# Two transformer blocks on one core: operands of block products made in steps, a last chunk of six tiles, and ten 4 kB weight tiles

## The chip, the cores and the metric

The kernel runs on one core of a Trainium2 chip. A core has a matrix engine (PE, with its weight loads shown as PEld), a vector engine (DVE), a scalar engine (ACT), a general engine (POOL) and a queue engine (SP) that issues most DMAs. The metric is the device time of one execution in microseconds. Matmul results land in PSUM; everything else lies in SBUF, 128 partitions wide.

## The reference

Two transformer blocks in float32 on one sequence of 512 tokens, width 1024. The change touches only the two feed-forward parts of the first block and the tiles that all weights go through:

```python
def swiglu(x, w1, w3, w2):
    return (jax.nn.silu(x @ w1) * (x @ w3)) @ w2

# first block, D_MODEL 1024, D_FF 2816
f = swiglu(rms_norm(h, ffn1_pre_g), ffn1_w1, ffn1_w3, ffn1_w2)
h = h + 0.5 * rms_norm(f, ffn1_post_g)
# sparse attention, short convolution, gates and merge ("mix")
# cross attention over 256 memory rows ("cross")
f = swiglu(rms_norm(h, ffn2_pre_g), ffn2_w1, ffn2_w3, ffn2_w2)
h = h + 0.5 * rms_norm(f, ffn2_post_g)
# second block: two attentions ("mix2"), an MLP ("mlp"), a gated part ("ple"), a final norm
```

## The kernel before, in words

Everything is kept transposed: a feature tile is 128 features by 512 tokens, so h is 8 tiles. A float32 product is made from three matmuls: each operand is split into a high part (a cast to a reduced float on ACT) and a low part (a subtraction on DVE), and `mm3` multiplies high by high, high by low, and low by high.

**Weights.** `load` (lines 241 to 251) takes a raw weight tile by DMA (tag `r4`, three tiles of 4 kB), casts it on ACT (line 249) and subtracts on DVE (line 250) into two tiles of tag `w4` (eight tiles of 4 kB, so four pairs). `lead_weights` (lines 262 to 282) loads the first weights of a phase through `r4` too, but puts the parts into slots of the pools `u` and `b`. The pools of working tiles have 32 (`b`), 8 (`t`) and 5 (`u`) slots of 2 kB, and 16 for split inputs (`x`).

**A feed-forward part** (`ffn`, lines 666 to 734). `enter` and `begin` turn h into split inputs xs and a row r of reciprocal norms, the token halves A and B one after the other; the first products run per half as their inputs come. The hidden width of 2816 is 22 tiles, taken in chunks of 4, 4, 4, 4, 4 and 2. For the first chunk the products with w1 and w3 are plain: four are made in `begin` (five in the second feed-forward part), the rest in `stream`, 24 matmuls each. `up` gives each hidden tile two `t` slots and a pair of `b` slots (u). Then `forms` (lines 359 to 398) makes the seven operands of the block products from h, the gain and r: four scaled blocks of h and three sums of them, each split in high and low parts, in slots of `t` (raw values), `b` and `x` (parts). It takes 16 scalings (line 368), 8 sums (line 375), 14 casts (line 381) and 14 subtractions (line 382). All other chunks use `fast` (line 424): a product of two tiles at a time by a scheme with seven instead of eight half-size block products. `blocks` (lines 400 to 422) makes its weights: two loads (`one` in `r4`, `two` in `r6`), differences (lines 412 to 414, `three` in `r4`, `four` in `r2`), and parts in `w4` and, for `four`, `w2` (lines 419 and 420).

After each chunk `down` multiplies its u tiles by w2 into eight result tiles f: eight products of 12 matmuls for a chunk of four, of 6 for a chunk of two. The first chunk's results are copied (line 661), the others added (line 659). In the last chunk the last five of the eight products (four in the second feed-forward part) run in halves: the A halves at once, the B halves kept in `self.rest`, which `begin` of the next phase issues between its own first steps.

**Order.** The program is written as one stream of operations, and a planner puts them in order on each engine: among what is ready in its plan it takes what stands first in the program, and it hands out the tiles of a tag as they come free. Each engine then runs its list strictly in order. So a subtraction that stands behind others on DVE waits for them, whoever needs it. SP's list of loads is in order too: a load whose raw tile isn't free holds those behind it.

Each phase names by `K["lead:..."]` the pools of its leading weights: `ubbbb` is one product's parts in `u` and four products' in `b`.

Of the kernel before, what the change touches and what calls it, by code (L numbers as in the profile page):

```python
# [11 lines left out]
F32 = mybir.dt.float32  # L12
F32R = mybir.dt.float32r
I32 = mybir.dt.int32
AF = mybir.ActivationFunctionType
OP = mybir.AluOpType
# [3 lines left out]
P = 128  # L20
D = 1024
KD = D // P
S = 512
# [3 lines left out]
KF = FF // P  # L27
# [29 lines left out]
HALVES = (A, B)  # L57
# [12 lines left out]
 'lo:mix': [6],  # L70
 'lo:mix2': [],
 'work': ['a', 'a', 'a', 'b', 'vK', 'V', '0', '1', '2', '3', 'bb', 'b', 'b', '', '', 'b'],
 'sizes:ffn1': [4, 4, 4, 4, 4, 2],
 'sizes:ffn2': [4, 4, 4, 4, 4, 2],
 'plain': 4,
 'urg:ffn1sf': 0,
 'sq:ffn1sf': 'PV',
# [90 lines left out]
 'oa': 'VVVVVVVV'}  # L168
BANKS = {k: v for k, v in K["banks"].items() if v}
SLOTS = dict(zip("btu", K["slots"]))  # L170
WEIGHTS = {"r6": 2, "r4": 3, "r2": 1, "w4": 8, "w2": 2}


def width(tok):
# [3 lines left out]
class Net:  # L178
    def __init__(self, ctx, tc, a):
# [6 lines left out]

        self.wp = {t: pool(t, n) for t, n in WEIGHTS.items()}

# [152 lines left out]
        for do in todo:  # L341
            do()

    def stream(self, jobs, tail=0, spare=0):

        mid = len(jobs) - tail
        for w, n, xs, k0, put in jobs[:mid]:
            put(self.lin(self.weights(w, n, len(xs), k0)[0], xs), ALL)  # L350
        wts = [self.lead_weights(w, n, len(xs), k0, "x") if i < spare else self.weights(w, n, len(xs), k0)[0]
               for i, (w, n, xs, k0, _) in enumerate(jobs[mid:])]
        for (_, _, xs, _, put), wt in zip(jobs[mid:], wts):
            put(self.lin(wt, xs, A), A)
            self.rest.append(lambda xs=xs, put=put, wt=wt: put(self.lin(wt, xs, B), B))
# [2 lines left out]

    def forms(self, gain, r):

        nc, h = self.nc, self.h
        two = lambda alloc, dt: [alloc((P, S), dt).rearrange("p (k t) -> p k t", k=2) for _ in range(2)]
        out = {}

        def scaled(c, half, alloc=self.tmp):
            t, tok = two(alloc, F32), HALVES[half]
            for k in range(4):
                nc.vector.scalar_tensor_tensor(  # L368
                    t[k // 2][:, k % 2], h[4 * c + k][:, tok], self.g(gain, 4 * c + k), r[:, tok], op0=OP.mult, op1=OP.mult)
            return t  # L370

        def combined(x, y, op):
            t = two(self.tmp, F32)
            for o, i, j in zip(t, x, y):
                nc.vector.tensor_tensor(o, i, j, op=op)
            return t

        def parts(name, src, alloc):
            hi, lo = two(alloc, F32R), two(alloc, F32R)
            for t, i, j in zip(src, hi, lo):  # L380
                nc.scalar.copy(i, t)
                nc.vector.tensor_tensor(j, t, i.bitcast(F32), op=OP.subtract)
            out[name] = [(hi[k // 2][:, k % 2], lo[k // 2][:, k % 2]) for k in range(4)]


        b11, b12 = scaled(0, 0), scaled(0, 1)
        t1 = combined(b11, b12, OP.subtract)
        parts("11", b11, self.big)
        b21 = scaled(1, 0, lambda shape, dt: self.big(shape, dt))
        parts("21", b21, self.big)  # L390
        b22 = scaled(1, 1)
        t2 = combined(b22, t1, OP.subtract)
        parts("1", t1, self.big)
        parts("2", t2, self.xt)
        parts("22", b22, self.xt)
        parts("3", combined(b22, b12, OP.add), self.xt)
        parts("4", combined(b21, t2, OP.subtract), self.xt)
        return out

    def blocks(self, w, n):  # L400

        nc, src = self.nc, self.a[w]
        c = 4 * P

        def tiles(tag, m):
            return self.weight(tag, m * c).rearrange("p (b c) -> p b c", c=c)

        one, two, three, four = tiles("r4", 2), tiles("r6", 3), tiles("r4", 2), tiles("r2", 1)

        nc.sync.dma_start(one, src[n].rearrange("p (b k) c -> p b (k c)", b=2))  # L410
        nc.sync.dma_start(two[:, 0:2], src[n + 1].rearrange("p (b k) c -> p b (k c)", b=2))
        nc.vector.tensor_tensor(two[:, 2], two[:, 0], one[:, 0], op=OP.subtract)
        nc.vector.tensor_tensor(three, two[:, 1:2].to_broadcast([P, 2, c]), two[:, 0::2], op=OP.subtract)
        nc.vector.tensor_tensor(four[:, 0], one[:, 1], three[:, 1], op=OP.subtract)
        out = []
        for tag, raw in (("w4", one), ("w4", three), ("w2", four), ("w4", two[:, 1:3])):
            m = raw.shape[1]
            hi, lo = tiles(tag, m), tiles(tag, m)
            nc.scalar.copy(hi, raw)  # L419
            nc.vector.tensor_tensor(lo, raw, hi.bitcast(F32), op=OP.subtract)  # L420
            out += [[(hi[:, b, k * P : k * P + P], lo[:, b, k * P : k * P + P]) for k in range(4)] for b in range(m)]
        return dict(zip(("11", "12", "1", "2", "4", "22", "3"), out))
# [226 lines left out]
        self.nc.scalar.dma_start(t, self.a[name])  # L649
        return t  # L650

    def down(self, w, f, k0, xs, add, late=(0, 0)):

        nc = self.nc

        def put(n):
            def go(ps, tok):
                if add:
                    nc.vector.tensor_tensor(f[n][:, tok], f[n][:, tok], ps, op=OP.add)
                else:  # L660
                    nc.scalar.copy(f[n][:, tok], ps)
            return go

        self.stream([(w, n, xs, k0, put(n)) for n in range(KD)], *late)

    def ffn(self, pre, post, w1, w3, w2):
        self.phase = post[:4]
        nc = self.nc
        xs, r, step = self.enter(pre)
        f = [self.big(dt=F32) for _ in range(KD)]  # L670

        def up(n):
            t1, t3, u = self.tmp(), self.tmp(), self.pair()

            def first(ps, tok):
                nc.vector.tensor_tensor(t1[:, tok], ps, r[:, tok], op=OP.mult)
                nc.scalar.activation(t1[:, tok], t1[:, tok], AF.Silu)

            def second(ps, tok):
                nc.vector.tensor_tensor(t3[:, tok], ps, r[:, tok], op=OP.mult)  # L680
                nc.gpsimd.tensor_tensor(t3[:, tok], t3[:, tok], t1[:, tok], op=OP.mult)
                self.split(t3[:, tok], [t[:, tok] for t in u])

            return u, [(w1, n, xs, 0, first), (w3, n, xs, 0, second)]

        def up2(n):

            t1, t3, u = ([self.tmp(), self.tmp()] for _ in range(2)), None, [self.pair(), self.pair()]
            t1, t3 = t1

            def first(i, tok, ps, t):
                if t is not None:
                    nc.vector.tensor_tensor(t1[i][:, tok], t, ps, op=OP.add)
                if i == 0 and tok == A:
                    return
                src, at = (t1[i], ALL) if i == 0 else (t1[i], tok)
                nc.scalar.activation(t1[i][:, at], ps if t is None else src[:, at], AF.Silu)

            def second(i, tok, ps, t):
                if t is None:  # L700
                    nc.vector.tensor_tensor(t3[i][:, tok], t1[i][:, tok], ps, op=OP.mult)
                else:
                    nc.vector.tensor_tensor(t3[i][:, tok], t, ps, op=OP.add)  # L703
                    if i == 0 and tok == A:
                        return
                    at = ALL if i == 0 else tok
                    nc.vector.tensor_tensor(t3[i][:, at], t3[i][:, at], t1[i][:, at], op=OP.mult)  # L707
                if i == 0 or t is None:
                    self.split(t3[i], u[i])

            return u, [(w1, n, first), (w3, n, second)]

        c = 0
        b = None
        for size in K["sizes:" + self.phase]:
            us, jobs, quick = [], [], []
            plain = K["plain"] if c == 0 else 0
            for n in range(c, c + plain):
                u, j = up(n)
                us.append(u)  # L720
                jobs += j
            if c == 0:
                self.begin(jobs[:K["ahead:" + self.phase]], step)
                jobs = jobs[K["ahead:" + self.phase]:]
                self.stream(jobs)
                b = self.forms(pre, r)
            for n in range(c + plain, c + size, 2):
                u, j = up2(n)
                us += u
                quick += j  # L730
            self.fast(quick, b)
            self.down(w2, f, c, us, c > 0, K["late:" + self.phase] if c + size == KF else (0, 0))
            c += size
        self.leave(f, post)

# [837 lines left out]
```

## Time and profile before

| | |
|---|---|
| three runs | 2169.66 us median, 2167.13 to 2172.68 |
| profiled execution | 2171.57 us, span 2169.8 us |
| PE busy | 2056.6 us (95%), 11852 matmuls |
| weight loads (PEld) | 1774.4 us (82%) |
| DVE busy | 1488.0 us (69%), 2869 instructions |
| ACT busy | 1031.5 us (48%) |
| POOL busy | 252.0 us (12%) |
| granted PE clock, mean | 0.971 of full |
| HBM read | 182.25 MB, 85 GB/s over the span |

The first feed-forward part takes about the first 375 us of the span, "mix" follows until about 760 us, "cross" until about 940 us, the second feed-forward part until about 1318 us, and the second block the rest. A row of the timeline gives start, duration, engine, line, operation, output from input, form and count of a run of like instructions, and in brackets how long the engine had stood idle before and what released it. Names are tiles: `mm` and `lg` are PSUM banks, `b`, `t`, `u`, `x` slots of the pools, `w` a split weight, `r` a raw one, `h` the residual, `rows` a broadcast row such as r. A row of the windows gives a stretch, its length, busy time and count for PE, PEld, DVE, ACT and POOL, and then the granted PE clock, the DMA share and GB/s.

### The profile page before, as it was taken

Reading aid. Unit: us, or ns where it says so; the run is one execution under the profiler, and the core shown is the slowest. Engines: PE = TensorE matmul, PEld = TensorE weight load, DVE = VectorE, ACT = ScalarE, POOL = GpSimd, SP = SyncE. Lnnn points to the kernel's source line nnn. Section 1 sums busy time; section 2 is a strip of 40 time slices with the busy share of each in tenths; the row PEclk is TensorE's granted clock in tenths of the full one; section 3 lists DMA queues with packets and bytes.
Section 4 is the critical chain, followed back from the end, with each engine's and each line's share of the span. In section 5 each row is a group of like instructions: output and inputs, shape, how many; then the busy total and the mean of one; then the engine's idle time right before and its main releaser. Section 6 shows DMA issues by size and latency. Waiting matters only on the chain.

```text
span 2169.8 us, 30997 instructions
## 1 busy us (share of the span) xinstructions
PE 2056.6 (95%) x11852; PEld 1774.4 (82%) x11852; DVE 1488.0 (69%) x2869; ACT 1031.5 (48%) x1877; POOL 252.0 (12%) x239
## 2 busy tenths in 40 slices
PE   8799999899999989987999997998999999999997
PEld 7699998778778878986999997876778888888887
DVE  5777777799775575475777769578987663443565
ACT  5444444673563553453544445467864432222352
POOL 2000000413331310030000003122110000000011
PEclk9999999799999989988999998999999999999999
DMA  5233333212313242220333323111012323223321
GB/s 162 73 98 105 101 107 114 77 59 88 96 61 97 69 141 83 78 69 28 104 108 107 98 76 119 59 45 49 30 49 79 119 65 97 97 88 97 106 98 40
DMA packets 67157, 186.36 MB, mean 86 GB/s; under 512 B 7104, under 2 KB 16320, under 8 KB 67008
## 3 DMA queue, kind: packets, MB, share of 16 engines
q1 hardware_dynamic: 64528, 180.97, 26.5%
q10 hardware_dynamic: 2448, 3.41, 0.5%
q8 instruction: 93, 1.52, 0.3%
q14 instruction: 56, 0.46, 0.1%
q0 software_dynamic: 32, 0.00, 0.0%
HBM read 182.25 MB, written 2.10 MB: 85 GB/s over the span
## 4 chain that ended last, share of the span: by engine, by line
PE 85%; DVE 8%; ACT 3%; issue 2%; POOL 2%; DMA 0%; SPq 0%; ACTq 0%; POOLq 0%; DVEq 0%
PE mm L287 44%; PE lg L287 34%; DVE h L592 1%; PE tt L820 1%; PE tt L544 1%; PE o L834 1%; PE o L835 1%; POOL b L890 1%; PE lg L785 1%; PE lg L786 1%; DVE t L368 1%; DVE b L591 1%; DVE w L250 0%; DVE x L476 0%; ACT w L249 0%
## 5 line engine op out<-in xcount | busy, mean ns | idle before, releaser
L287 PE MATMUL mm<-x,w 128*128 128x512 f32 (+1 forms) x2808 | 606.4, 366 | 0.5 <-DVE w L250 0.5
L287 PEld LDWEIGHTS mm<-x,w 128*128 128x128 f32 x2808 | 476.2, 189 | 90.2 <-DVE w L250 1.0
L249 ACT CAST w<-r 128x1024 fp32r<-128x1024 f32 (+2 forms) x290 | 258.8, 893 | 486.5 <-PE mm L287 221.7
L287 PE MATMUL mm<-b,w 128*128 128x512 f32 (+1 forms) x2253 | 413.7, 334 | 23.2 <-ACT w L249 20.3
L287 PEld LDWEIGHTS mm<-b,w 128*128 128x128 f32 x2253 | 337.9, 190 | 74.0 <-ACT w L249 21.5
L250 DVE TENSOR_TENSOR w<-r,w 128x1024 fp32r<-128x1024 f32 (+2 forms) x288 | 297.6, 1034 | 113.6 <-ACT w L249 106.0
L287 PE MATMUL lg<-x,w 128*128 128x256 f32 (+1 forms) x2304 | 365.7, 312 | 0.0
L287 PE MATMUL lg<-b,w 128*128 128x512 f32 (+1 forms) x1725 | 342.3, 349 | 6.6 <-DVE w L250 6.4
L287 PEld LDWEIGHTS lg<-x,w 128*128 128x128 f32 x2304 | 319.8, 188 | 33.1 <-DVE t L703 2.0
L287 PEld LDWEIGHTS lg<-b,w 128*128 128x128 f32 x1725 | 279.4, 192 | 53.2 <-DVE w L250 7.8
L419 ACT CAST w<-r 128x1024 fp32r<-128x1024 f32 (+1 forms) x144 | 135.1, 945 | 111.2 <-PE mm L287 50.3
L420 DVE TENSOR_TENSOR w<-r,w 128x1024 fp32r<-128x1024 f32 (+1 forms) x144 | 155.5, 1087 | 22.7 <-ACT w L419 21.1
L472 ACT CAST b<-t 128x512 fp32r<-128x512 f32 (+1 forms) x100 | 58.7, 587 | 114.8 <-DVE t L707 33.5
L531 POOL TENSOR_TENSOR sf<-sf,sf 128x256 f32<-128x256 f32 x28 | 21.6, 771 | 788.8 <-ACT sf L525 768.5
L531 POOL TENSOR_TENSOR sh<-sh,sh 128x256 f32<-128x256 f32 x45 | 36.4, 809 | 529.0 <-ACT sh L525 526.0
L525 ACT ACTIVATE sh<-h 128x256 f32<-128x256 f32 x128 | 49.9, 411 | 51.7 <-DVE h L592 19.8
L473 DVE TENSOR_TENSOR b<-t,b 128x512 fp32r<-128x512 f32 (+1 forms) x100 | 64.2, 642 | 14.8 <-ACT b L472 14.3
L287 PE MATMUL mm<-x,b 128*128 128x256 f32 x456 | 70.2, 300 | 2.9 <-DVE t L892 2.3
L890 POOL TENSOR_TENSOR b<-b,rows 128x512 f32<-128x512 f32 x32 | 52.3, 1635 | 174.9 <-ACT b L888 174.9
L823 DVE TENSOR_TENSOR u<-tt,u 128x512 fp32r<-128x512 f32 x92 | 61.9, 683 | 13.1 <-ACT u L822 12.5
L287 PE MATMUL lg<-x,b 128*128 128x256 f32 x456 | 69.1, 295 | 0.0
L287 PEld LDWEIGHTS mm<-x,b 128*128 128x128 f32 x456 | 63.7, 206 | 3.5 <-DVE t L892 2.6
(262 smaller groups left out, 2533.4 us busy)
## 6 DMA issues: line engine op xcount, KB each, us to landing
r<-in_ffn_w SPq DMA_DIRECT2D x86, 512.0 KB, 3.6
r<-in_w_in SPq DMA_DIRECT2D x64, 512.0 KB, 3.5
r<-in_ffn_w SPq DMA_DIRECT2D x84, 256.0 KB, 2.7
r<-in_w_up SPq DMA_DIRECT2D x32, 512.0 KB, 3.5
r<-in_w_down SPq DMA_DIRECT2D x32, 512.0 KB, 3.8
r<-in_w_out SPq DMA_DIRECT2D x8, 512.0 KB, 3.4
r<-in_xattn_w_k SPq DMA_DIRECT2D x8, 512.0 KB, 3.8
r<-in_xattn_w_v SPq DMA_DIRECT2D x8, 512.0 KB, 4.1
```

The source lines that it names most:

```text
L249: nc.scalar.copy(hi, raw)
L250: self.second.tensor_tensor(lo, raw, hi.bitcast(F32), op=OP.subtract)
L287: self.nc.tensor.matmul(ps, lhsT=lhsT, rhs=rhs, start=start, stop=stop, skip_group_check=on)
L368: nc.vector.scalar_tensor_tensor(t[k // 2][:, k % 2], h[4 * c + k][:, tok], self.g(gain, 4 * c + k), r[:, tok], op0=OP.mult, op1=OP.mult)
L419: nc.scalar.copy(hi, raw)
L420: nc.vector.tensor_tensor(lo, raw, hi.bitcast(F32), op=OP.subtract)
L472: nc.scalar.copy(hi, src)
L473: nc.vector.tensor_tensor(lo, src, hi.bitcast(F32), op=OP.subtract)
L525: nc.scalar.activation(t, x, AF.Square)
L531: eng.tensor_tensor(ts[0], ts[0], t, op=OP.add)
L823: nc.vector.tensor_tensor(lo, ps[:, :n], hi.bitcast(F32), op=OP.subtract)
L890: nc.gpsimd.tensor_tensor(t[:, tok], t[:, tok], r[:, tok], op=OP.mult)
```

## The change

`forms` no longer makes all operands at once behind the plain products. It returns two lists of steps. The first six (scaled block and its sum, and the third scaled block, for each pair of tiles) are run by `stream` between the last plain products, the other eight between the eight products of the first `down`. The sums are made in place in the tiles of the raw scaled blocks, so that eight `t` slots hold all raw values. The last two chunks, of 4 and 2 tiles, become one of 6. The weight tiles become two of tag `r6`, two of `r4` and ten of `w4`; `four` and its two parts are put in slots of the pool `u`.

```diff
- 'sizes:ffn1': [4, 4, 4, 4, 4, 2],
- 'sizes:ffn2': [4, 4, 4, 4, 4, 2],
+ 'sizes:ffn1': [4, 4, 4, 4, 6],
+ 'sizes:ffn2': [4, 4, 4, 4, 6],
...
-WEIGHTS = {"r6": 2, "r4": 3, "r2": 1, "w4": 8, "w2": 2}
+WEIGHTS = {"r6": 2, "r4": 2, "w4": 10}
...
-    def stream(self, jobs, tail=0, spare=0):
+    def stream(self, jobs, tail=0, spare=0, steps=()):
         mid = len(jobs) - tail
-        for w, n, xs, k0, put in jobs[:mid]:
+        for i, (w, n, xs, k0, put) in enumerate(jobs[:mid]):
             put(self.lin(self.weights(w, n, len(xs), k0)[0], xs), ALL)
+            for _ in range(-(-len(steps) // (mid - i))):
+                steps.pop(0)()
...
     def forms(self, gain, r):
...
+        def scaled(i, kk, half):
+            t, tok = two(self.tmp, F32), HALVES[half]
+            for k in range(2):
+                n = 4 * i + 2 * kk + k
                 nc.vector.scalar_tensor_tensor(
+                    t[:, k], h[n][:, tok], self.g(gain, n), r[:, tok], op0=OP.mult, op1=OP.mult)
             return t
+        def parts(name, kk, src, alloc):
             hi, lo = two(alloc, F32R), two(alloc, F32R)
+            nc.scalar.copy(hi, src)
+            nc.vector.tensor_tensor(lo, src, hi.bitcast(F32), op=OP.subtract)
...
+        def sum_into(a, b, x, op):
+            nc.vector.tensor_tensor(raw[a], raw[b], raw[x], op=op)
+        def make(kk):
+            x, y, z, w = ((n, kk) for n in "xyzw")
+            def b11():
+                raw[x] = scaled(0, kk, 0)
+                parts("11", kk, raw[x], self.big)
+            def t1():
+                raw[y] = scaled(0, kk, 1)
+                sum_into(x, x, y, OP.subtract)
+                parts("1", kk, raw[x], self.big)
+            def b21():
+                raw[w] = scaled(1, kk, 0)
+                parts("21", kk, raw[w], self.big)
+            def b22():
+                raw[z] = scaled(1, kk, 1)
+                parts("22", kk, raw[z], self.xt)
...
+            return [b11, t1], [b21], [b22, t3, t2, t4]
+        (a, b, c), (d, e, f) = make(0), make(1)
+        return out, a + d + b + e, c + f
...
     def blocks(self, w, n):
-        one, two, three, four = tiles("r4", 2), tiles("r6", 3), tiles("r4", 2), tiles("r2", 1)
+        single = lambda dt: self.slot("u", (P, c), dt).rearrange("p (b c) -> p b c", c=c)
+        one, two, three, four = tiles("r4", 2), tiles("r6", 3), tiles("r4", 2), single(F32)
...
-            hi, lo = tiles(tag, m), tiles(tag, m)
+            hi, lo = (tiles("w4", m) if m > 1 else single(F32R) for _ in range(2))
...
-                self.stream(jobs)
-                b = self.forms(pre, r)
+                b, early, steps = self.forms(pre, r)
+                self.stream(jobs, steps=early)
...
-            self.down(w2, f, c, us, c > 0, K["late:" + self.phase] if c + size == KF else (0, 0))
+            self.down(w2, f, c, us, c > 0, K["late:" + self.phase] if c + size == KF else (0, 0), steps)
```

More of the change, by code (lines that the diff above doesn't have):

```diff
@@ L361, in forms, with two @@
         nc, h = self.nc, self.h
[L362 to L367, printed above, removed]
+        out = {n: [None] * 4 for n in ("11", "21", "22", "1", "2", "3", "4")}
+        raw = {}
+        def two(alloc, dt):
+            return alloc((P, S), dt).rearrange("p (k t) -> p k t", k=2)
+        def scaled(i, kk, half):
+            t, tok = two(self.tmp, F32), HALVES[half]
+            for k in range(2):
+                n = 4 * i + 2 * kk + k
@@ L368, in scaled @@
                 nc.vector.scalar_tensor_tensor(
-                    t[k // 2][:, k % 2], h[4 * c + k][:, tok], self.g(gain, 4 * c + k), r[:, tok], op0=OP.mult, op1=OP.mult)
+                    t[:, k], h[n][:, tok], self.g(gain, n), r[:, tok], op0=OP.mult, op1=OP.mult)
             return t
[L372 to L378, printed above, removed]
-            hi, lo = two(alloc, F32R), two(alloc, F32R)
[L380 to L383, printed above, removed]
@@ L386, in forms @@
[L386 to L397, printed above, removed]
@@ L398, in forms, with t3, t2, t4 @@
-        return out
+        def parts(name, kk, src, alloc):
+            hi, lo = two(alloc, F32R), two(alloc, F32R)
+            nc.scalar.copy(hi, src)
+            nc.vector.tensor_tensor(lo, src, hi.bitcast(F32), op=OP.subtract)
+            for k in range(2):
+                out[name][2 * kk + k] = hi[:, k], lo[:, k]
+        def sum_into(a, b, x, op):
[15 more added lines that the diff above has]
+                parts("22", kk, raw[z], self.xt)
+            def t3():
+                sum_into(y, z, y, OP.add)
+                parts("3", kk, raw[y], self.xt)
+            def t2():
+                sum_into(z, z, x, OP.subtract)
+                parts("2", kk, raw[z], self.xt)
+            def t4():
+                sum_into(w, w, z, OP.subtract)
+                parts("4", kk, raw[w], self.xt)
+            return [b11, t1], [b21], [b22, t3, t2, t4]
@@ L415, in blocks @@
         out = []
-        for tag, raw in (("w4", one), ("w4", three), ("w2", four), ("w4", two[:, 1:3])):
+        for raw in (one, three, four, two[:, 1:3]):
             m = raw.shape[1]
-            hi, lo = tiles(tag, m), tiles(tag, m)
+            hi, lo = (tiles("w4", m) if m > 1 else single(F32R) for _ in range(2))
             nc.scalar.copy(hi, raw)
@@ L650, in table, with down @@
         return t
-    def down(self, w, f, k0, xs, add, late=(0, 0)):
+    def down(self, w, f, k0, xs, add, late=(0, 0), steps=()):
         nc = self.nc
@@ L662, in put @@
             return go
-        self.stream([(w, n, xs, k0, put(n)) for n in range(KD)], *late)
+        self.stream([(w, n, xs, k0, put(n)) for n in range(KD)], *late, steps)
     def ffn(self, pre, post, w1, w3, w2):
```

## The prediction

> **What bounds the kernel now.** I read the page's busy shares first, then the waits of PE, longest first, then PE's timeline around the longest, and DVE's beside it.
>
> ```profile
> PE 2056.6 (95%) x11852; PEld 1774.4 (82%) x11852; DVE 1488.0 (69%) x2869; ACT 1031.5 (48%) x1877; POOL 252.0 (12%) x239
> PE mm L287 <- ACT w L249: 20.3, 2, 10.2
> ```
>
> PE is busy 95% of the span, so only its 113 us of gaps, and what its clock loses after them, can be won without fewer products, and the change keeps the products. The longest wait comes twice, 10 us each: once in each of the two feed-forward blocks. PE there (start, duration, count, idle before):
>
> ```profile
> 58.97 2.26 PE L287 MATMUL mm<-b,w 128*128 128x512 f32 x9
> 62.10 0.50 PE L287 MATMUL mm<-b,w 128*128 128x512 f32 x1 [0.88 <-ACT b L472]
> ...
> 79.28 0.80 PE L287 MATMUL mm<-b,w 128*128 128x512 f32 x1 [10.15 <-ACT w L249]
> 80.52 4.21 PE L287 MATMUL lg<-b,w 128*128 128x512 f32 x10 [0.44 <-DVE w L250]
> ...
> 92.73 4.33 PE L287 MATMUL lg<-b,w 128*128 128x512 f32 x24
> ...
> 1003.72 2.26 PE L287 MATMUL mm<-b,w 128*128 128x512 f32 x9
> ...
> 1024.03 0.79 PE L287 MATMUL mm<-b,w 128*128 128x512 f32 x1 [10.15 <-ACT w L249]
> ...
> 1037.82 4.38 PE L287 MATMUL lg<-b,w 128*128 128x512 f32 x24
> ```
>
> This is the first call of `down` (eight products of 12 matmuls). PE stands after three of them for want of split weights. What DVE does meanwhile:
>
> ```profile
> 42.98 0.68 DVE L250 TENSOR_TENSOR w<-r,w 128x512 fp32r<-128x512 f32 x1
> ...
> 59.17 0.69 DVE L680 TENSOR_TENSOR t<-lg,rows 128x512 f32<-128x512 f32 x1 [4.31 <-PE lg L287]
> 59.77 2.69 DVE L368 SCALAR_TENSOR_TENSOR t<-h,gains,rows 128x256 f32<-128x256 f32 x4
> ...
> 79.19 0.67 DVE L382 TENSOR_TENSOR x<-t,x 128x512 fp32r<-128x512 f32 x1
> 79.79 0.67 DVE L250 TENSOR_TENSOR w<-r,w 128x512 fp32r<-128x512 f32 x1
> ```
>
> From 59.77 to 79.8 it works through `forms` (L368, L375, L382); the low weight parts for `down` (L250) queue behind. Just before, it idled 4.31 us, in the last plain product. The granted clock (next to last but two column) of the gap, of the stretch after it, and of a stretch of block products:
>
> ```profile
> 69.00:79.20 10.20, 0.13 (x1) 0.00 (x0) 10.20 (x20) 7.54 (x14) 0.00 (x0) 0.74 0.00 0
> 80.50:84.70 4.20, 4.18 (x11) 3.33 (x12) 3.07 (x5) 0.62 (x1) 0.00 (x0) 0.57 0.53 157
> 100.00:110.00 10.00, 10.00 (x89) 9.81 (x88) 7.86 (x11) 5.37 (x10) 0.00 (x0) 1.00 0.32 107
> ```
>
> After the gap PE runs at 0.57 for 4.2 us; in the block products it never stands, with DVE at 79%.
>
> **The change part by part.** The sum stands against the profiled execution's 2171.6 us (span 2169.8), 1.9 above the median of the three runs (2169.7).
>
> (a) `forms` in steps. The instruction count stays: 16 scalings (L368), 8 sums (L375), 14 casts on ACT, 14 subtractions (L382), no DMA. Prices, start to start, from the chain of waits:
>
> ```profile
> 63.07 1.58 DVE t L368 x4
> 64.66 1.20 DVE t L375 x2
> 65.86 0.60 DVE b L382
> ...
> 87.30 2.80 PE lg L287 x12
> ```
>
> So 16 x 0.40 + 8 x 0.60 + 14 x 0.60 = 19.6 us of DVE. Six steps (9.6 us: two of 1.4, two of 2.0, two of 1.4) now go between the last plain products; these last 5.6 us each, and DVE has 22.4 us there (16.8 in the second block), with some nine rows of its own of 0.7 us (L676, L680, L473, L250). Eight steps (10.0 us) go between the products of the first `down`. Can DVE keep up there? From 59.2: the put 0.6, one early step whose slot only now comes free 1.4 (two in the second block, 2.8), u's low part 0.6, four weight parts 2.4, late steps 10.0, and of the first block products' weights L412 to L414 and one low part, 3.7: 18.7 us (20.1) against PE's 0.9 + 8 x 2.80 = 23.3. It fits with 3 to 5 us spare, so PE need not stand. With ten 4 kB tiles the weights of four products, not three, are split when `down` begins: 11.2 us of cover. ACT has per product a cast 0.6, a copy 0.6 and a step's cast 0.6 in 2.8.
>
> Today `down` lasts from 58.97 to 92.73 + 2.80 = 95.53: 36.6 us for 22.4 of work, so 14.2 lost, the slow clock in it; in the second block 1003.72 to 1040.62, 14.5 lost. The 0.88 us for the last u stays, as its chain (L680, POOL, ACT) does. With 0.5 us each kept back for a step that stands in front of a weight part, 12.8 + 13.1 = **25.9 us** gained. Ends: nothing is won if the steps land in one lump before the weights, 28.7 if even the u wait goes.
>
> (b) Last chunk of six. Per block eight products of 12 and eight of 6 matmuls become eight of 18: PE the same. Removed are eight adds on DVE (L659, 128x512), eight loads, and the fixed part of eight casts and subtractions. PE has no gap in that stretch; zero, hidden by PE, and if that cover were gone it would be a gain. What moves is at the end: the last five (second block: four) products run in token halves, and the second halves fill PE while the first half's norm goes through DVE. The gaps there:
>
> ```profile
> 365.20 0.87 PE L287 MATMUL lg<-b,w 128*128 128x256 f32 x6
> 365.90 0.87 PE L287 MATMUL mm<-b,w 128*128 128x256 f32 x6
> ...
> 378.44 0.66 PE L555 MATMUL tt<-ident,r 128*128 128x128 f32 x2 [4.61 <-DVE r L505]
> 378.90 1.71 PE L544 MATMUL tt<-ones,sf 128*128 128x1 f32 x8
> ...
> 385.05 0.58 PE L287 MATMUL lg<-x,u 128*128 128x256 f32 x1 [4.45 <-ACT x L475]
> ...
> 410.47 3.39 PE L287 MATMUL mm<-x,u 128*128 128x256 f32 x19 [2.47 <-DVE t L749]
> ...
> 1322.25 0.66 PE L555 MATMUL tt<-ident,r 128*128 128x128 f32 x2 [3.97 <-DVE r L505]
> ...
> 1327.17 0.58 PE L287 MATMUL mm<-x,u 128*128 128x256 f32 x1 [2.77 <-ACT x L475]
> ```
>
> A half of 6 matmuls takes 0.70 us, so 12 more in each of five halves put 7.0 us of work behind the first half's last product (5.6 in the second block). The norm starts that much earlier, against gaps of 9.1 and 6.7 us. But DVE is nearly full in this stretch, and the 12 u tiles keep `b` slots: 8 (f) + 12 + 3 (tables) + 16 (lead weights) = 39 of 32, where 31 were used, so the last lead weights wait for the second halves. I take 6 + 4 = **10 us**; ends 15.8 (all gaps) and -3 (two products' lead weights, late by four casts and subtractions of 0.6).
>
> The trace prices what is left: after a gap of only 2.47 us, at 410.47, 19 matmuls took 3.39 us instead of 2.2, so a gap that shrinks to 2 or 3 us still costs 1 us of clock, which is why I take less than the filler. The Trainium skill (TensorE: Matmul & The Clock Gate, "Why this matters for your kernels") puts the limit at gaps above some 3 us. This trace contradicts it at 2.47 us; by that rule the rest would stay at full clock and (b) would be 12, the time 2 us lower.
>
> (c) Ten 4 kB tiles (five pairs, were four), two raw tiles (were three). Where PE waits for a low part:
>
> ```profile
> 788.63 5.07 PE L287 MATMUL lg<-b,w 128*128 128x256 f32 x22 [5.53 <-DVE w L250]
> ...
> 941.77 0.51 PE L287 MATMUL lg<-x,u 128*128 128x256 f32 x2 [1.26 <-DVE x L476]
> ...
> 944.12 0.48 PE L287 MATMUL lg<-x,u 128*128 128x256 f32 x1 [1.85 <-ACT x L475]
> ```
>
> At 788.63 one more ready pair is one product of 24 (2.8 us) more cover; at 941 five pairs let all first halves run before any second half. I take **4 us**; ends 9 and, as fewer raw tiles may deliver later, -4. At the start the third raw load is issued before any subtraction is done with the first:
>
> ```profile
> 5.92 1.38 SPq L270 DMA_DIRECT2D r<-in_ffn_w  x3
> ...
> 8.82 0.68 DVE L280 TENSOR_TENSOR u<-r,u 128x512 fp32r<-128x512 f32 x1
> ```
>
> With two it waits on SP until 9.5, with x's second half queued behind it or put ahead: **+1 us** (0 to 3).
>
> (d) `four` and its parts from `u`: three of five slots, with no other user during block products. Zero; PE at 100% hides it.
>
> Sum: 2171.6 - 25.9 - 10 - 4 + 1 = 2132.7; less the 1.9 to the median, **2131 us**.
>
> **Rivals.** (1) The steps stay a lump. `forms` began right behind the last L680 although DVE was free before, so something in the order of the slots held it; if it holds the early steps too, DVE has 9.6 - 1.4 = 8.2 us more after 59.2, 26.9 against 23.3: 3.6 us of gap and 1.3 of clock per block, 10 in all: 2141. Against it: each step's tiles are now first used between the products, ahead of the last put's. (2) The tail wins nothing, since DVE and the `b` slots bind: 2141, with the lead weights late 2144. For it speaks DVE at work without a break there.
>
> (3) Slower: the raw tiles. `blocks` holds both for `one` and `three`:
>
> ```profile
> r<-in_ffn_w SPq DMA_DIRECT2D x86, 512.0 KB, 3.6
> ...
> 168.35 0.69 DVE L412 TENSOR_TENSOR r<-r,r 128x512 f32<-128x512 f32 x1 [2.02 <-DMA r<-in_ffn_w]
> ...
> 169.29 1.22 DVE L420 TENSOR_TENSOR w<-r,w 128x1024 fp32r<-128x1024 f32 x1
> ...
> 176.00 0.68 DVE L414 TENSOR_TENSOR r<-r,r 128x512 f32<-128x512 f32 x1
> ```
>
> Landing 3.6, L412 0.7, L413 and one low part 1.2 each, L414 0.7: 7.4 us until `one`'s tile is free, against 84 matmuls, 9.5 us, per call: hidden. If L414 stays as late as here, 7.6 us after L412, it is 3.6 + 7.6 + 0.7 + 1.2 = 13.1, 3.6 over; with half of that, 1.8 us in each of 36 calls, 65 us: 2196. It decides from 1.1 us a call. Against it: L414 is late because `four` has one slot; now it has more. The Trainium skill (Perfetto Trace Analysis, "Optimization Strategy") reads the same gap repeated on the engine that should be full as too few buffers; today no such gap shows in the block products. (4) The order is planned anew and most is given back elsewhere: 2155 to 2168.
>
> **How the numbers follow.** Forecast 0.57 (its own range 2114 to 2139), (1) 0.10, (2) 0.18, (3) 0.07, (4) 0.08. The range 2114 to 2152 leaves out (3), (4) and a little at the bottom. A difference under 0.3% (6.5 us) can't be told from none: faster 0.89, same 0.04, slower 0.07.
>
> **What would show it.** Right: no PE wait on L249 near 79 and 1024, `down` at 24 us, clock 1.0 there; L368 spread among L676 and L680; shorter gaps before L555 and the first x product. Wrong: L368 in one run behind the last L680; PE waiting on L420 in block products; a new wait on L279 or L280 at the start of the next block.

## The result and the profile after

The changed kernel takes 2120.51 us (median, 2115.4 to 2124.0) against 2169.19 us for the kernel before on the same chip: a ratio of 0.9772 [0.9748, 0.9796], 49 us less. The forecast was 2131 us with a range of 2114 to 2152. Lines up to 343 keep their numbers; those of `forms` become L377 (scalings), L389 (sums), L383 (casts), L384 (subtractions), and what lies behind them moves by 30 (L412 is L442, L505 is L535, L680 is L710).

The page's first part, and the waits of PE, longest first (total, times, longest):

```profile
span 2119.2 us, 31071 instructions
PE 2047.0 (97%) x11960; PEld 1775.7 (84%) x11960; DVE 1481.9 (70%) x2837; ACT 1024.4 (48%) x1861; POOL 252.8 (12%) x239
PE mm L287 <- ACT x L505: 6.7, 2, 5.8
PE tt L574 <- DVE sh L561: 6.3, 2, 5.4
```

The 10.15 us wait on L249, twice in the kernel before, is gone, and so are most of those before L555. What now leads the list was there before or stands in a new place (the wait on L561, below). PE's gaps went from 113 us to 72 us, so 41 of the 51 us of span are gaps; the rest is PE's own busy time, with the mean granted clock up from 0.971 to 0.984.

PE's timeline at the two first calls of `down` (start, duration, count, idle before):

```profile
59.20 2.26 PE L287 MATMUL mm<-b,w 128*128 128x512 f32 x9
62.34 0.50 PE L287 MATMUL mm<-b,w 128*128 128x512 f32 x1 [0.88 <-ACT b L502]
...
79.94 4.38 PE L287 MATMUL lg<-b,w 128*128 128x512 f32 x24
...
972.22 2.26 PE L287 MATMUL mm<-b,w 128*128 128x512 f32 x9
976.06 0.50 PE L287 MATMUL mm<-b,w 128*128 128x512 f32 x1 [0.88 <-ACT b L502]
...
993.05 4.33 PE L287 MATMUL lg<-b,w 128*128 128x512 f32 x24
```

The last row ends at 79.94 + 2.80 = 82.74: 23.5 us for the eight products, where 36.6 were needed, and 23.6 in the second block. One gap is left, the 0.88 us for the last u. DVE beside it, and a window over the place of the old gap (PE, PEld, DVE, ACT and POOL busy, then the granted clock, DMA share, GB/s):

```profile
43.21 1.67 DVE L377 SCALAR_TENSOR_TENSOR t<-h,gains,rows 128x256 f32<-128x256 f32 x4
...
48.81 2.70 DVE L377 SCALAR_TENSOR_TENSOR t<-h,gains,rows 128x256 f32<-128x256 f32 x4
...
60.01 2.69 DVE L377 SCALAR_TENSOR_TENSOR t<-h,gains,rows 128x256 f32<-128x256 f32 x4
...
75.29 0.69 DVE L384 TENSOR_TENSOR x<-t,x 128x512 fp32r<-128x512 f32 x1
...
77.76 1.22 DVE L450 TENSOR_TENSOR w<-r,w 128x1024 fp32r<-128x1024 f32 x1
...
68.90:79.90 11.00, 11.00 (x49) 8.87 (x48) 10.67 (x17) 8.49 (x13) 0.00 (x0) 1.00 0.25 72
```

Scalings now stand at 43 and 48 us, where DVE stood idle before (for 4.31 us in front of its instruction at 47.97, and for 1.83 us in front of that at 51.09); of the six early steps only the last is left behind the last L710, which ends at 60.0. DVE is busy 10.67 of 11.00 us in the window and still in time: the low part of the first block product's weights ends at 78.98, and PE starts on it at 82.74.

To see where the gain arose, I took the start of the first product of a stage in the profiled executions of both kernels, and from stage to stage the change in their distance. Positive is time won, in us, and a second profiled execution of the changed kernel stands below the first (up to 1.6 us apart in a stage). Stages that an edit doesn't touch move by up to 3.7 us ("five late halves" changes only ffn2, and its end of ffn1 reads 1.1), so less than 4 us in one stage is no finding, but for the two columns of `forms`, which agree within 0.1 us in every kernel that runs the steps in their place. One execution of "all but six" took 4159 us, and no figure below uses it:

```
                 start  forms,  end of  mix to  forms,  end of  rest   all
                        ffn1    ffn1    ffn2    ffn2    ffn2
changed          -0.2   +12.9    +4.8   +14.0   +13.4    +5.8   -0.1  +50.6
 once more       -0.7   +13.0    +3.2   +14.1   +13.4    +4.3   +0.5  +47.8
steps only       -0.1   +12.9    +1.9    +2.5   +13.4    -0.9   -0.8  +28.9
six only         -2.4    -0.9    -1.6    +4.0    +0.3    +9.0   -0.8   +7.5
tiles only       +0.1    +2.8    -1.0   +14.9    +3.0    -4.6   +1.1  +16.1
all but tiles    -2.0   +12.9    -4.7    +4.1   +13.4    +5.0   +0.3  +29.1
all but six      -1.9   +12.9    +0.4   +18.2   +13.4    -4.7   +1.3  +39.5
steps in a lump  -2.4    +8.9    +5.1   +16.9    +9.5    +5.7   -0.8  +42.9
chunk of eight   -1.5   +13.0    +7.7   +15.2   +13.4    +6.1   +0.6  +54.6
 once more       +0.4   +13.0    +5.9   +15.7   +13.4    +5.4   +0.2  +54.1
five late halves -0.1   +12.9    +1.1   +15.7   +13.4    +5.9   +0.2  +49.2
one raw fewer    -0.4    -0.1    +0.6    -0.5    +0.1    -3.3   +0.5   -3.2
```

### The profile page after: what moved, and what is told of

It is laid out like the page before. It is cut to its first block, busy times and chain, and to the rows that moved or that the text cites. A ratio compares the mean times of both kernels' runs of the same rounds, so it can differ in the third digit from the quotient of the medians.

```text
span 2119.2 us, 31071 instructions
## 1 busy us (share of the span) xinstructions
PE 2047.0 (97%) x11960; PEld 1775.7 (84%) x11960; DVE 1481.9 (70%) x2837; ACT 1024.4 (48%) x1861; POOL 252.8 (12%) x239
## 5 line engine op out<-in xcount | busy, mean ns | idle before, releaser
L287 PE MATMUL mm<-x,w 128*128 128x512 f32 (+1 forms) x2376 | 549.6, 382 | 0.0
L287 PEld LDWEIGHTS mm<-x,w 128*128 128x128 f32 x2376 | 423.5, 189 | 89.1 <-DVE v L1266 0.7
L249 ACT CAST w<-r 128x1024 fp32r<-128x1024 f32 (+2 forms) x274 | 256.0, 935 | 453.5 <-PE mm L287 194.3
L287 PE MATMUL mm<-b,w 128*128 128x256 f32 (+1 forms) x2313 | 409.1, 329 | 2.1 <-ACT b L502 1.8
L287 PE MATMUL lg<-b,w 128*128 128x512 f32 (+1 forms) x1773 | 332.4, 339 | 0.0
L449 ACT CAST w<-r 128x1024 fp32r<-128x1024 f32 x108 | 113.5, 1053 | 77.3 <-PE lg L287 48.2
L450 DVE TENSOR_TENSOR w<-r,w 128x1024 fp32r<-128x1024 f32 x108 | 131.2, 1221 | 7.9 <-ACT w L449 7.7
L287 PE MATMUL mm<-x,u 128*128 128x256 f32 x600 | 94.7, 301 | 14.6 <-ACT x L505 6.7
L287 PEld LDWEIGHTS mm<-x,u 128*128 128x128 f32 x600 | 84.4, 206 | 17.5 <-ACT x L505 7.2
L561 POOL TENSOR_TENSOR sh<-sh,sh 128x256 f32<-128x256 f32 x45 | 36.9, 820 | 517.2 <-ACT sh L555 514.3
L561 POOL TENSOR_TENSOR sf<-sf,sf 128x256 f32<-128x256 f32 x28 | 23.3, 832 | 456.8 <-ACT sf L555 446.6
L555 ACT ACTIVATE sh<-h 128x256 f32<-128x256 f32 x128 | 50.0, 411 | 52.0 <-DVE h L622 24.1
```

What stands on the lines that cost most here:

```text
L287: self.nc.tensor.matmul(ps, lhsT=lhsT, rhs=rhs, start=start, stop=stop, skip_group_check=on)
L555: nc.scalar.activation(t, x, AF.Square)
L561: eng.tensor_tensor(ts[0], ts[0], t, op=OP.add)
```

## The experiments

**The three parts one by one.** Each of these is the kernel before with one part of the change. First the steps alone:

```diff
-                self.stream(jobs)
-                b = self.forms(pre, r)
+                b, early, steps = self.forms(pre, r)
+                self.stream(jobs, steps=early)
...
-            self.down(w2, f, c, us, c > 0, ...)
+            self.down(w2, f, c, us, c > 0, ..., steps)
```

> The kernel before with the operands made in steps and nothing else (old chunks, old weight tiles). Theory (each part pays for itself): the two first calls of down lose their 10 us gap and the slow clock after it, 13.0 + 13.3 = 26.3 us as in the changed kernel, since 18.7 us of DVE work fit beside 23.3 us of PE whether three or four products stand ready: 2143 us, down from 59 in about 23.5 us, no wait of PE on L249 there. Rival (the ten tiles carry part of it): with only three products' weights ready, the fourth stands behind the steps, and 3 us of gap per block stay: 2150 us.

Measured: 2142.63 us, ratio 0.9889 [0.9873, 0.9906]. By the table 12.9 and 13.4 us come from the two first calls of `down`, as in the changed kernel, with four pairs of weight tiles instead of five. PE's timeline there:

```profile
76.97 2.96 PE L287 MATMUL mm<-b,w 128*128 128x512 f32 x12
79.77 4.38 PE L287 MATMUL lg<-b,w 128*128 128x512 f32 x24
```

The eight products now run through at full clock, with no gap but the 0.87 us for the last u. The steps carry their gain alone, and the fourth product that the ten tiles keep ready is not needed for it.

The last chunk of six alone:

```diff
- 'sizes:ffn1': [4, 4, 4, 4, 4, 2],
- 'sizes:ffn2': [4, 4, 4, 4, 4, 2],
+ 'sizes:ffn1': [4, 4, 4, 4, 6],
+ 'sizes:ffn2': [4, 4, 4, 4, 6],
```

> The kernel before with the last chunk of six and nothing else. Theory: 12 more matmuls in each second half fill PE at the two block ends, 4.7 + 5.9 = 10.6 us as in the changed kernel: 2158.5 us. Rival: with four pairs of weight tiles the fifth product's weights wait for a second half, so the first halves can't run through; 4 to 6 us only: 2164 us. Rival from the b slots: nothing is won: 2169 us.

Measured: 2161.95 us, ratio 0.9974 [0.9963, 0.9986]. That fits the rival of 4 to 6 us (2164 of 2169 us is a ratio of 0.9976) and not the theory (2158.5 us, 0.9951). The end of ffn2, with four late products, wins 9.0 us; the end of ffn1, with five, wins nothing. PE there:

```profile
412.60 0.55 PE L287 MATMUL mm<-x,u 128*128 128x256 f32 x1 [7.19 <-DVE t L749]
```

The wait for the second halves, on L749, grew from the 2.47 us shown at 410.47 to 7.19 us.

The ten weight tiles alone, with `four` in `u`:

```diff
-WEIGHTS = {"r6": 2, "r4": 3, "r2": 1, "w4": 8, "w2": 2}
+WEIGHTS = {"r6": 2, "r4": 2, "w4": 10}
```

> The kernel before with the new weight tiles (two raw of 4 kB, ten for parts, four and its parts in u) and nothing else. Theory (the pairs pay in every phase): 14 us between the first feed-forward part and the second, as in the changed kernel, and with a fourth product ready before each first down 2.8 us less gap twice: 2149.5 us, the 10.15 us waits down to about 7.3. Rival (the 14 us came with the shifted order of the changed kernel, not with the pairs): only the 5.6 us: 2163.5 us. Rival (one raw tile fewer costs): 2175 us or more.

Measured: 2155.0 us, ratio 0.9941 [0.9926, 0.9956], between the theory and the first rival: both gains that the theory named are there, and a loss that it did not name. By far the most is won between attention and ffn2, 14.9 us. The old gap in `down` remains, cut in two:

```profile
74.21 1.22 PE L287 MATMUL mm<-b,w 128*128 128x512 f32 x2 [2.80 <-ACT b L663]
79.23 0.80 PE L287 MATMUL lg<-b,w 128*128 128x512 f32 x1 [3.80 <-ACT w L249]
```

One pair more gives one product more of cover and no more: 2.8 and 3.0 us. The end of ffn2 loses 4.6 us.

**All but the tiles.** The changed kernel with three raw and eight weight tiles:

```diff
-WEIGHTS = {"r6": 2, "r4": 2, "w4": 10}
+WEIGHTS = {"r6": 2, "r4": 3, "w4": 8}
```

> The changed kernel with three raw tiles and eight tiles for parts (four and its parts stay in u). Theory (the pairs pay 14 us between the feed-forward parts): 2120.5 + 14 = 2134.5 us, with a gap near 780 as before the change. Rival (they do not): 2120 us.

Measured: 2141.68 us, ratio 0.9882 [0.9866, 0.9897], 0.0110 above the changed kernel's, 24 us (21.5 by the profiled executions), more than the 14 expected. PE's waits in question:

```profile
401.70 0.55 PE L287 MATMUL mm<-x,u 128*128 128x256 f32 x1 [7.18 <-DVE t L779]
...
779.72 4.54 PE L287 MATMUL lg<-b,w 128*128 128x256 f32 x22 [5.54 <-DVE w L250]
```

The wait of 5.5 us on a low weight part is back, and so is the 7.2 us in front of ffn1's second halves. The tiles are worth 10 us between attention and ffn2, and 6 to 9.5 us at the end of ffn1 (by the three executions that have both), where the chunk of six without them loses. Some 2 us more lie at the start, and are no work of the tiles (last section).

**All but the chunk of six.** The changed kernel with the old sizes, 4, 4, 4, 4, 4 and 2.

> The changed kernel, with the old chunk sizes (4, 4, 4, 4, 4, 2), so that the late halves at the end of each feed-forward block are 6 matmuls long again, not 18. Theory: the last chunk of six is worth about 10 us once there are five pairs of weight tiles (4.7 us in the end of the first block, 5.9 us in that of the second): 2131 us; the sum of the steps alone (26.0) and the tiles alone (13.6) gives 2129. Rival: the five pairs alone already let the first halves run through, and the longer halves add nothing: 2120.5 to 2123 us.

Measured: 2135.75 us, ratio 0.9838 [0.9824, 0.9851]. That lies above both expectations: beside the five pairs the chunk of six is worth some 14 us by the ratios (0.9838 less 0.9772, of 2170; the intervals leave 8 to 20) and 11.1 by the profiled executions, where 10 were expected. PE at the ends of ffn1 and ffn2:

```profile
369.53 0.66 PE L585 MATMUL tt<-ident,r 128*128 128x128 f32 x2 [3.99 <-DVE r L535]
...
377.14 0.58 PE L287 MATMUL lg<-x,u 128*128 128x256 f32 x1 [5.46 <-ACT x L505]
...
403.16 1.10 PE L287 MATMUL mm<-x,u 128*128 128x256 f32 x7 [3.30 <-DVE t L779]
...
1284.45 0.66 PE L585 MATMUL tt<-ident,r 128*128 128x128 f32 x2 [4.71 <-DVE r L535]
...
1291.62 0.58 PE L287 MATMUL mm<-x,u 128*128 128x256 f32 x1 [4.99 <-ACT x L505]
```

The last two are 9.7 us at the end of ffn2, where the kernel before had 6.7. That five pairs let the short first halves run out earlier, so that PE stands longer, is my reading; no run separates it. But at the ends the two parts need each other. By the table the two ends together give +7.4 us with six alone, -5.6 with the tiles alone, and +10.6 (7.5 the second time) with both; with the steps and the six but without the tiles they give +0.3.

**Steps in a lump.** The changed kernel, with the six early steps written behind the plain products:

```diff
-                self.stream(jobs, steps=early)
+                self.stream(jobs)
+                for go in early:
+                    go()
```

> The changed kernel, with the six early steps of forms written behind the last plain product instead of between these products (the eight late steps stay between the products of down). Theory (the prediction's first rival as a mechanism): slots and VectorE's order follow the order in which the program first uses the tiles, so VectorE stays idle between the plain products and the 9.6 us of early steps stand in front of down's last weight parts: about 3.6 us of gap and 1.3 us of slow clock in each of the two blocks, 10 us in all over the changed kernel's 2120.5, 2130.5 us. Rival A: VectorE takes the early steps as soon as it is free, wherever they are written: 2120.5 us, no change. Rival B: without the early steps between the products nothing of (a) is left: 26 us, 2146.5 us.

Measured: 2128.81 us, ratio 0.9802 [0.9786, 0.9817]; 0.0030 above the changed kernel's, 6.5 us (7.6 by the profiled executions). The intervals just overlap; they don't against the second measurement of the changed kernel, 0.9761 [0.9748, 0.9775], shown below. DVE, then PE:

```profile
61.54 0.69 DVE L710 TENSOR_TENSOR t<-lg,rows 128x512 f32<-128x512 f32 x1 [4.31 <-PE lg L287]
62.15 2.69 DVE L377 SCALAR_TENSOR_TENSOR t<-h,gains,rows 128x256 f32<-128x256 f32 x4
...
76.08 2.60 PE L287 MATMUL mm<-b,w 128*128 128x512 f32 x10 [1.78 <-DVE w L250]
...
80.45 0.50 PE L287 MATMUL mm<-b,w 128*128 128x512 f32 x1 [1.31 <-ACT w L249]
```

DVE stands idle for 4.31 us again, with its inputs at hand, and begins the scalings only behind the last L710. So where the steps are written decides when they run, which kills the rival that DVE takes them as it comes free. Whether it is the planner's order or the tile slots that hold them back, no run separates. The price is the two gaps, 1.78 + 1.31 = 3.1 us per block, where 3.6 and 1.3 of slow clock were expected; the clock stays at full speed behind them (ten matmuls in 2.60 us). The table's 4.0 holds 0.9 us of block products that this kernel puts ahead of the mark.

**One raw tile fewer.** The kernel before with `r4` 2 in place of 3, nothing else.

> The kernel before, with two raw tiles of 512 KB instead of three and nothing else changed (four keeps its one slot). It tests the prediction's slower rival by itself. Rival: the raw load of one call waits until L414 of the call before has freed one's tile, and with four's single slot L414 stays as late as in the trace of before, 7.6 us after L412; that is 3.6 us over the 9.5 us of a call, in each of 36 calls, 130 us, or 65 us with half of it: 2235 to 2300 us. Theory: L414 moves forward by itself when loads come later, since VectorE has time over in the block products; only the start loses up to 1 us: 2168 to 2172 us.

Measured: 2174.71 us, ratio 1.0012 [1.0003, 1.0021]: 2.6 us slower, not 65 or more. DVE at the call of `blocks` that the prediction shows, and at the next:

```profile
166.32 0.68 DVE L412 TENSOR_TENSOR r<-r,r 128x512 f32<-128x512 f32 x1
...
168.30 0.69 DVE L414 TENSOR_TENSOR r<-r,r 128x512 f32<-128x512 f32 x1
...
176.69 0.68 DVE L412 TENSOR_TENSOR r<-r,r 128x512 f32<-128x512 f32 x1
...
179.69 0.68 DVE L414 TENSOR_TENSOR r<-r,r 128x512 f32<-128x512 f32 x1
```

L414 now comes 2.0 and 3.0 us behind L412, where it came 7.6 us behind (5.5 us in the call before that one): DVE had room, and with one raw tile fewer the order shifted by itself. `four`'s single slot was not what kept it late. The stage distances show no loss in the block products; the 3.3 us lost at the end of ffn2 lie within what stages move by themselves.

**Further variants.** Five late halves at the end of ffn2 (`'late:ffn2': [5, 0]`):

> The changed kernel, with five products in halves instead of four at the end of the second feed-forward block (the first has five already); a fifth pair of weight tiles is there for it. Theory: one more half of 18 matmuls, 2.1 us, fills most of the gaps of 0.8, 0.95 and 1.18 us there: 2 us less, 2118.5 us. Rival: VectorE is the one that is late there (the second half's gap of 2.35 us moves by as much): 2120.5 us, no change.

Measured: 2121.22 us, ratio 0.9774 [0.9759, 0.9789]: no difference. A gain of 2 us could not be told by the ratio, but the distance there, +5.9 us against +5.8 and +4.3, shows none either, as the rival said. Then chunks of 4, 4, 6 and 8 (`'sizes:ffn1': [4, 4, 6, 8]`, ffn2 alike):

> The changed kernel, with chunks of 4, 4, 6 and 8 tiles: late halves of 24 matmuls, so 3.5 us more work behind the first half's last product (2.8 us in the second block), and eight rounds of adds fewer per block. Theory: what gaps are left between the first halves' norm and the next product (0.8 + 2.4 us in the first block, 0.8 + 2.1 us in the second) are filled by it, the gap in front of the second half (4.4 us) is not: 4 us less, 2116.5 us. Rival: sixteen u tiles leave too few slots for the lead weights (8 + 16 + 3 + 16 = 43 of 32), some of which come late: 5 us per block more, 2130 us.

Measured: 2118.06 us, ratio 0.9767 [0.9754, 0.9781]. Neither the lost 5 us per block nor clearly the gain of 4. So both were run side by side:

> The changed kernel itself, on the same chip as the next run, for the comparison of the two: 2121 us, 0.977 of before.

> The changed kernel with chunks of 4, 4, 6 and 8 tiles, beside the changed kernel itself. By the spans of the profiled runs so far it is 4 us shorter (2115.2 against 2119.2 us): 2117 us. Rival: that difference is the spread of single runs, and longer halves win nothing more: 2121 us, the same.

Measured: the changed kernel 2119.53 us, ratio 0.9761 [0.9748, 0.9775]; the chunk of eight 2117.47 us, ratio 0.9754 [0.9741, 0.9767]. The intervals overlap nearly whole; a gain of some 2 us is possible and is not shown.

## Why the prediction was right, and where it was not

The total came 10.5 us below the forecast, inside the range, and nearly all of that is one term, (c). By the terms of the sum:

**(a) Steps: 25.9 us forecast, 26.3 measured** (12.9 + 13.4 by the table, in both executions of the changed kernel and with the steps alone; 24 us by the ratio of the steps alone). The cover worked out for DVE held, too: 18.7 us of work against 23.3 gave 4.6 to spare, and the trace shows 82.74 - 78.98 = 3.8. The u wait stayed at 0.88 us, as said. The reserve of 0.5 us per block was hardly needed (23.5 us against 23.3). The cover of a fourth ready product, which the prediction counted in, was not needed: the steps alone won as much with three. The first rival did not come about. Written as a lump the steps do what it feared, shown by running it; its 10 us were 6.5.

**(b) Chunk of six: 10 us forecast, 10.6 and 7.5 measured in two executions.** The size is right, but partly by luck, for the account was not complete. PE at the two ends:

```profile
358.54 0.40 PE L585 MATMUL tt<-ident,r 128*128 128x128 f32 x2 [0.80 <-DVE r L535]
...
370.07 0.39 PE L287 MATMUL lg<-x,u 128*128 128x256 f32 x1 [1.05 <-ACT x L505]
...
391.12 0.55 PE L287 MATMUL mm<-x,u 128*128 128x256 f32 x1 [4.43 <-DVE t L779]
...
1274.55 0.40 PE L585 MATMUL tt<-ident,r 128*128 128x128 f32 x2 [0.76 <-DVE r L535]
...
1299.19 4.52 PE L287 MATMUL mm<-x,b 128*128 128x256 f32 x24 [2.35 <-DVE t L922]
```

The gaps of 4.61 and 4.45 us became 0.80 and 1.05; but the gap in front of the second halves went from 2.47 to 4.43 us, and the sum did not have it. What the prediction held back for, the `b` slots, did not show: with 16 u tiles (43 slots wanted of 32) the kernel was no slower. And the step treated (b) and (c) as independent, while at the end of ffn1 the six lose without the fifth pair (-4.7 us, all but tiles) and the fifth pair wins nothing there without the six (-1.0, +0.4). Six alone are worth 5.6 us by the ratio, and taken out of the changed kernel 14.

**(c) Ten weight tiles: 4 us forecast, 14 measured** between attention and ffn2. Not all 14 need be the tiles': alone they win 14.9 us there, and the changed kernel without them keeps 4.1, so that they add 10. This is the term that was mis-sized, beyond even its end of 9. Windows of both handovers (the end of mix into cross, and cross into ffn2) and rows of PE's timeline, of the kernel before (the first two numbers behind the length are PE's and PEld's busy time, the third from last is the granted clock):

```profile
762.40:782.70 20.30, 18.78 (x134) 18.50 (x134) 17.39 (x42) 11.96 (x25) 5.76 (x7) 0.83 0.41 130
...
788.60:794.00 5.40, 5.37 (x25) 5.37 (x26) 3.39 (x5) 2.21 (x4) 0.00 (x0) 0.50 0.63 197
...
915.10:1003.70 88.60, 79.78 (x546) 74.45 (x545) 49.23 (x111) 36.30 (x83) 24.38 (x28) 0.92 0.16 48
...
762.46 1.50 PE L544 MATMUL tt<-ones,sh 128*128 128x1 f32 x10 [0.28 <-DVE sh L531]
763.99 5.06 PE L287 MATMUL mm<-b,w 128*128 128x256 f32 x22
...
891.65 0.38 PE L820 MATMUL tt<-ident,t 128*128 128x128 f32 x2
...
967.53 0.95 PE L287 MATMUL mm<-x,u 128*128 128x256 f32 x5 [2.81 <-DVE x L476]
969.69 1.83 PE L544 MATMUL tt<-ones,sh 128*128 128x1 f32 x8 [1.20 <-DVE sh L533]
```

The same two handovers in the changed kernel, and what is left of the gaps:

```profile
742.00:762.00 20.00, 19.34 (x170) 19.31 (x170) 17.18 (x43) 10.78 (x23) 6.23 (x7) 1.00 0.45 146
...
767.50:773.50 6.00, 5.94 (x19) 5.14 (x20) 4.38 (x14) 2.34 (x4) 0.00 (x0) 0.52 0.48 146
...
893.10:972.20 79.10, 76.39 (x522) 72.82 (x521) 54.73 (x122) 34.67 (x81) 24.23 (x28) 0.91 0.17 51
...
767.56 2.29 PE L574 MATMUL tt<-ones,sh 128*128 128x1 f32 x10 [5.41 <-DVE sh L561]
...
865.88 0.38 PE L850 MATMUL tt<-ident,t 128*128 128x128 f32 x2
...
915.09 0.35 PE L574 MATMUL tt<-ones,sf 128*128 128x1 f32 x2 [0.88 <-DVE sf L563]
...
936.82 1.56 PE L574 MATMUL tt<-ones,sh 128*128 128x1 f32 x8 [1.82 <-DVE sh L563]
```

From cross's last part to ffn2's `down` (the windows from 915.10 and 893.10) PE's idle time fell from 88.60 - 79.78 = 8.8 us to 2.7. These two windows hold all the gaps but not the same work (546 and 522 matmuls), so their lengths can't be compared. From the last transposes of cross (891.65 and 865.88) to the first `down` (1003.72 and 972.22) it is 112.1 us before and 106.3 after, 5.7 us less; without the tiles ("all but tiles") it is 111.8 us again. At the end of mix the 5.53 us in front of 788.63 are replaced by 5.41 us in front of 767.56, now for the norm of the second halves. But before, PE ran slow twice there: at 763.99, where 22 matmuls took 5.06 us (2.7 at full clock), and again at 788.63. Now it does so once: between the last transposes of mix and the first of cross the clock records show half clock for 17.1 us before and for 6.8 us now, while PE's idle time hardly changed, 8.9 us and 8.2. From the last transposes of mix to the last of cross that makes 6.1 us; the other 2.2 of the 14 lie inside mix.

The prediction quoted three rows here (788.63, 941.77, 944.12; 8.6 us) and took half. It left out the second handover's other gaps (967.53 and 969.69, 4.0 us), and the slow clock at 763.99, which no gap of note stands in front of. So what it named at 788 was only exchanged for another wait, and what it did not name was most of the gain. What fell short was to price a buffer by the gaps of three rows alone, without the clock.

**Start: +1 us forecast, 0.2 and 0.7 measured** up to the first `down`; the third raw load does wait, but PE does not need it earlier.

**(d)** held: PE shows no wait on `four` or its parts. The third rival fell with `before_r2`: the reading that L414 is late because `four` has one slot was false, and it would have been late only as long as nobody needed it early. The fourth rival is out by the total. The second is not, since (c) gave 10 us more than forecast and could hide a tail that wins nothing; it is out by the ends in the table and by the run without the chunk of six.

## What to carry to other kernels

Where each engine runs its list in order, as here, a piece of work starts where the program puts it, so an idle engine in front of a lump is a reason to cut the lump and write its pieces earlier; work out the cover as that engine's work against PE's between the two points, which here came out within 1 us. When a buffer is added, list all gaps of every handover that it can reach, with the slow clock behind each: the three rows that looked relevant were the smaller part of what it gave. Two parts that act at the same handover (longer filler, and the tiles to hold its weights) have to be priced together: alone, the one won nothing at the end of ffn1, and the other lost at the end of ffn2.

## What the runs showed of the hardware

The pace of the matmuls at the start changes between executions of one and the same program. Two of the kernel with the chunk of eight, on two chips, PE's timeline:

```profile
16.78 1.86 PE L287 MATMUL lg<-x,b 128*128 128x256 f32 x9
```

```profile
14.52 1.24 PE L287 MATMUL lg<-x,b 128*128 128x256 f32 x9
```

The same nine matmuls took 1.86 and 1.24 us; in the first the slow pace lasted until about 18 us, in the second until about 12. Yet the granted clock reads 1.00 in both from 5.8 us on. The traces' first clock records, to full clock, stand at 18.2 and 11.9 us; the column reads 1.00 where there is no record yet, so here the durations have to be read. The five rows of the table that lose 1.5 to 2.4 us at the start are just those whose first record comes at 18.2 to 19.9 us; in the other eight executions it comes at 11.9 to 13.8 us. So that loss is the clock's, and need not come from their edits. The Trainium skill (TensorE: Matmul & The Clock Gate, "What's actually happening") says that the activity window runs freely and that the warm-up varies from run to run; these two rows agree.

A gap's length alone did not decide what came behind it: a window of the kernel before, and then one of all but six, each right behind a gap (length, PE busy, granted clock):

```profile
410.50:413.80 3.30, 3.30 (x19) 0.69 0.00 0
```

```profile
403.10:405.00 1.90, 1.84 (x14) 1.00 0.00 0
```

Behind 2.47 us (410.47) PE ran at 0.69, behind 3.30 us (403.16) at 1.00; and at 763.99 it ran slow behind a gap of 0.28 us, with 20 matmuls of one column each (L544) in the 3.4 us ahead of it. The Trainium skill (the same page and section) names some 3.4 us of idle time as the limit, which fits the second of the three and neither of the others.

The clock records show what the gaps alone do not. In all 13 profiled executions the granted clock is 1.0 or 0.5, and within an execution it changes only at points that lie multiples of 3.413 us apart. For every such stretch of 3.413 us at full clock I counted the columns that PE's matmuls moved (512 for one of 128x512, one for one of 128x1, and one that runs across a border shared out; at the pace of 12 x 512 columns in 2.80 us a full stretch holds some 7490). All 144 falls to half clock come right behind a stretch with fewer than 3050 columns; of the 7629 stretches at full clock that no fall followed, four had fewer. The three cases fit. The stretch from 408.37, with the gap of 2.47 us in it, held 2600 columns; the one from 759.94, with the small matmuls, held 1100; and the gap of 3.30 us was spread over two stretches that still held 3100 and 3700. So where a gap lies counts as well as how long it is, and small gaps or small matmuls in one stretch add up. This is a count over the records of these kernels; no run moved a gap on purpose.
